# Spreading SSD decays and gate rows by DRAM reads instead of TensorE products, in a one-layer hybrid trunk

## The chip, the cores and the metric

The kernel runs on one core of one Trainium2 chip. A core has five engines that each work through their own list of instructions in order and wait for each other through semaphores: TensorE (PE in the profile, with its weight loads as PEld), VectorE (DVE), ScalarE (ACT), GpSimd (POOL) and SyncE (SP), which here only issues transfers. Transfers between DRAM, where the inputs lie, and the on-chip memory SBUF are done by DMA engines; PE writes its results into PSUM, a small memory of eight banks of 128 x 512 f32 values.

The metric is the device time of the whole kernel in microseconds (us). Before the change it is 1217.26 us, the median of 3 runs (1215.96 to 1217.44). "Time" always means this one number; positions such as "425 us" are microseconds from the start of the profiled execution's span.

## The reference

One layer of a hybrid encoder over 1024 positions of width 1024. What matters here is the state-space group (SSD, 8 heads of width 64) and how its output joins the residual:

```
z, xbc, dt_raw, q, k, v = split(h @ W_in)
dt    = softplus(dt_raw + dt_bias)                 # 1024 x 8
adt   = -exp(a_log) * dt
a_cs  = cumsum(adt) over each chunk
L     = exp(a_cs[l] - a_cs[s])  for s <= l, else 0  # one 'decay' matrix per chunk and head
y     = ((C B^T) * L) @ (xs * dt)                   # inside the chunk
      + exp(a_cs) * (C @ state_before)              # from earlier chunks
state = exp(a_cs[-1]) * state + B^T @ (exp(a_cs[-1] - a_cs) * xs * dt)
y     = (y + d_skip * xs) * silu(z)
y_ssd = y / rms(y) * norm_w
x     = x + g_m * (concat[y_ssd, y_att] @ W_out)    # g_m, g_f: one row of 1024 each, from c
x     = x + g_f * ffn(...)
```

The sequence is handled in 8 tiles of 128 positions, which the kernel calls chunks (c = 0 to 7). All values are f32. Large products are made of three products of a rounded high part and a low rest (names that end in h or H and l or L), so that the result has f32 precision.

## The kernel before, in words

The program runs through the layer once. The stretch that matters lies between about 370 and 525 us:

- **z tiles.** `z_tile(ch, st, wz)` computes columns of `h @ W_in` for tile `st`, first the half `ch = 1` (372 to 398 us, which also holds dt_raw), then the half `ch = 0` (398 to 423 us). PE makes 24 products of 260 columns, ACT and DVE then bring the result out of PSUM into `zs` (lines 656, 657 for half 1, 660, 661 for half 0, the last of which is z times the sigmoid part of silu). Half 0 needs the weights `wzh`, `wzl`, which are loaded and split on ACT and DVE between the halves (lines 82, 83).
- **Gate rows.** g_m and g_f exist as 128 x 8 columns `gcol`. Products by rows need them spread over all 128 partitions. `row_of` does that: DVE multiplies the identity by the columns (line 141), PE multiplies the result by a matrix of ones (line 144), ACT copies it out (line 145). It is called for g_m behind the first z tile and for g_f behind the third. The row of g_m is folded into four parts of W_out by DVE (`wout_fold`, line 612, tiles `wst`, `wos`); its other half stays as `gm1`. The row of g_f goes to DRAM as a full 128 x 1024 tile (`gfd`, line 852) and comes back near the end of the program.
- **dt_prep** (from 398.8 us) computes dt and adt (`sm_dt`, `sm_e`) on DVE and ACT, then three products of adt on PE with a lower triangle `tle`, a strict upper triangle `sgt` and ones, and one exp: `ex3` holds the three decays of 64 columns (`ea`, `de`, `cd`, one column per chunk and head).
- **ssd_pre(c)** makes what chunk c needs: `xdt = xs * dt` (DVE), `xdd = xdt * de` (POOL), the product C B^T (`cb`, masked by `tle`), and the decay matrices of 8 heads. For these, ACT and DVE multiply `tle` by each head's column of adt, high and low part apart (lines 714, 716, 720, tile `rm`), and PE multiplies by the strict triangle `sgtr` (tile `sg`, two products of 512 columns for each of two groups of four heads); ACT takes the exp (line 739) and DVE multiplies by `cb` (line 740, tile `th`).
- **ssd_y(c)** is PE's part: `ydp` (inside the chunk), `yop` (from the state), `stp` (the new state), with POOL making `yy = d_skip * xs` ahead (line 811) and DVE adding up (829 to 832).
- **ssd_norm(c)** multiplies by `zs` (DVE, 837), takes the mean square (ACT 839, POOL 116 and 117) and scales (ACT 841). **ssd_turn(c)** transposes the result on PE into `xps` and copies it into `xs`; `wout_rhs` splits it into `yhl`.
- **wout_half(n)** multiplies `yhl` by the split W_out (tiles `hH`, `hL`) into `wops`: 24 products of 512 columns. Half n of them runs beside chunk n: three steps between the two groups of ssd_pre(c + 1), the rest behind it. So PE's row in the loop is: ydp, yop, stp, turn of the chunk before, products of ssd_pre(c + 1), wops.

PE's order in the loop is the order in which the program writes it (`pe` chains each product to the one before). On the other engines a scheduler places each instruction by its own estimate; `issue_after` and the list `pin` only bound it: the split of W_out (`wout_split`) waits in the order for the instructions in `pin`. Buffers come from pools with a fixed number of copies: `rm` has 2, `xdt` and `xdd` 2 each, the SSD tiles in PSUM 3 banks (`PB`: banks for wops, xps, sg and SSD tiles).

## Time and profile before

| What | us |
| --- | --- |
| time, median of 3 runs | 1217.26 |
| the profiled execution's own time | 1219.3 |
| its span (first to last instruction) | 1217.5 |
| PE busy | 1170.7 |
| VectorE busy | 928.7 |
| ScalarE busy | 598.1 |
| GpSimd busy | 148.6 |
| z tiles, half 1 / half 0 | 372 to 398 / 398 to 423.4 |
| SSD loop, first ydp to the last turn | 425.13 to 521.34 |

All from one profiled execution, on the one core; its mean granted PE clock was 0.991 of full speed. In the rows of a timeline the columns are: start, duration, engine, line, operation, output<-inputs, shape, count of instructions joined in the row, and in brackets the idle time of the engine before it with what ended that. Where several instructions are joined the duration runs from the first start to the last end. PE's products overlap in their pipeline, so a product's own duration is longer than its distance to the next. In the view of waits a row says who waited for whom, in total, how often, and the longest. In the view of stretches each engine's busy time is followed by its count of instructions; the last three numbers are the granted clock, the share of busy DMA and GB/s. In the list of transfers the last number is the median time from issue to landing.

### The profile page before, as it was taken

To read this page: it belongs to the slowest core of one execution; us is meant where nothing else is said; L and a number is where in the kernel's file an instruction comes from. 1 tells how busy PE (TensorE), PEld (TensorE's weight loads), DVE (VectorE), ACT (ScalarE), POOL (GpSimd) and SP (SyncE) were. 2 spreads that over 40 slices of the span, in tenths; PEclk is the share of its full clock that TensorE was granted. 3 is DMA by queue.
4 is the path that set the end of the run, shared out by engine and by line. 5 is a ranking of instruction groups with operands and counts; after the bars stand their busy time and mean duration, and the time that the engine had idled before them with its cause. 6 is when DMAs were issued, how large, how long until landed. Compare 5 with 4: busy or idle time off the path is not lost.

```text
span 1217.5 us, 15642 instructions
## 1 busy us (share of the span) xinstructions
PE 1170.7 (96%) x5802; PEld 977.2 (80%) x5802; DVE 928.7 (76%) x1394; ACT 598.1 (49%) x1001; POOL 148.6 (12%) x174
## 2 busy tenths in 40 slices
PE   5998999989999999999999999999999999999996
PEld 3877887878788978888878888888888888888885
DVE  7846455686696678746999988988889869756986
ACT  4636454674333766676644533344334445433444
POOL 1202242440000134200000000000000000000522
PEclk9999999999999989999999999999999999999999
DMA  9612121311576201141223223322232277734443
GB/s 343 249 57 80 42 70 39 123 48 50 173 261 206 88 14 39 53 150 58 70 96 112 104 95 130 126 76 85 104 130 95 87 277 274 270 120 130 149 137 146
DMA packets 56395, 150.86 MB, mean 124 GB/s; under 512 B 5632, under 2 KB 5760, under 8 KB 54912
## 3 DMA queue, kind: packets, MB, share of 16 engines
q1 hardware_dynamic: 49264, 125.49, 30.5%
q10 hardware_dynamic: 7056, 24.38, 5.0%
q8 instruction: 45, 0.74, 0.2%
q14 instruction: 30, 0.25, 0.1%
HBM read 116.56 MB, written 29.10 MB: 120 GB/s over the span
## 4 chain that ended last, share of the span: by engine, by line
PE 70%; DVE 5%; ACT 1%; issue 1%; DMA 1%; POOL 0%; POOLq 0%; DVEq 0%; ACTq 0%; SPq 0%
PE wops L699 6%; PE dn L78 5%; PE dn L77 5%; PE dn L76 5%; PE uY L76 5%; PE uY L78 5%; PE uY L77 4%; PE uX L78 3%; PE uX L76 3%; PE uZ L77 3%; PE uZ L76 3%; PE uX L77 3%; PE uZ L78 3%; PE s L76 3%; PE s L77 3%; PE s L78 3%
## 5 line engine op out<-in xcount | busy, mean ns | idle before, releaser
L77 PE MATMUL dn<-w 128*128 128x512 f32 x296 | 108.1, 391 | 0.0
L76 PE MATMUL dn<-w 128*128 128x512 f32 x296 | 108.1, 391 | 0.0
L78 PE MATMUL dn<-w 128*128 128x512 f32 x296 | 100.2, 391 | 0.2 <-DVE w L86 0.2
L76 PE MATMUL uY<-tH,w 128*128 128x512 f32 x248 | 97.2, 392 | 0.0
L77 PE MATMUL uY<-tL,w 128*128 128x512 f32 x248 | 97.0, 391 | 0.0
L78 PE MATMUL uY<-tH,w 128*128 128x512 f32 x248 | 96.9, 391 | 0.0
L1427 POOL TENSOR_TENSOR ya<-ya,xs 128x512 f32<-128x512 f32 x4 | 17.2, 4338 | 557.7 <-ACT xs L1423 557.7
L85 ACT ACTIVATE w<-ya 128x1024 fp32r<-128x1024 f32 (+1 forms) x41 | 39.2, 956 | 87.3 <-PE uY L78 84.2
L699 PE MATMUL wops<-hH,yhl 128*128 128x512 f32 x224 | 75.9, 407 | 2.9 <-DVE yhl L86 1.5
L78 PEld LDWEIGHTS dn<-w 128*128 128x128 f32 x296 | 55.4, 188 | 13.2 <-DVE w L86 1.1
L76 PEld LDWEIGHTS dn<-w 128*128 128x128 f32 x296 | 55.5, 188 | 12.4
L77 PEld LDWEIGHTS dn<-w 128*128 128x128 f32 x296 | 55.5, 188 | 12.2
L413 DVE CUSTOM_DVE_ANT_0 p<-s,bias 128x640 f32<-128x640 f32 (+4 forms) x64 | 40.7, 652 | 25.0 <-PE tp L445 9.0
L85 ACT ACTIVATE w<-xs 128x1024 fp32r<-128x1024 f32 (+1 forms) x41 | 39.1, 953 | 37.3 <-PE uY L78 33.3
L419 POOL TENSOR_SCALAR p<-p,st 128x640 f32<-128x640 f32 (+4 forms) x64 | 46.1, 726 | 76.7 <-DVE st L418 66.5
L86 DVE TENSOR_TENSOR pt<-tp,pt 128x512 fp32r<-128x512 f32 (+2 forms) x72 | 42.0, 595 | 16.9 <-ACT pt L85 16.5
L78 PEld LDWEIGHTS uY<-tH,w 128*128 128x128 f32 x248 | 46.6, 188 | 10.4
L76 PEld LDWEIGHTS uY<-tH,w 128*128 128x128 f32 x248 | 46.6, 188 | 10.4
L77 PEld LDWEIGHTS uY<-tL,w 128*128 128x128 f32 x248 | 46.6, 188 | 10.2
L699 PEld LDWEIGHTS wops<-hH,yhl 128*128 128x128 f32 x224 | 42.9, 193 | 12.5 <-DVE yhl L86 1.9
L76 PE MATMUL s<-hH,wh 128*128 128x512 f32 x128 | 50.2, 392 | 1.6 <-DVE ct L520 1.6
L1101 DVE SCALAR_TENSOR_TENSOR a<-cv,pkt,a 128x1023 f32<-128x1023 f32 (+1 forms) x40 | 50.9, 1276 | 0.1
(459 smaller groups left out, 3430.5 us busy)
## 6 DMA issues: line engine op xcount, KB each, us to landing
wos<-in_w_ada_dram SPq DMA_DIRECT2D x25, 512.0 KB, 4.7
gz<-a ACTq DMA_DIRECT2D x10, 1024.0 KB, 4.9
ya<-in_w_up_dram SPq DMA_DIRECT2D x11, 768.0 KB, 4.2
xs<-in_w_up_dram SPq DMA_DIRECT2D x11, 768.0 KB, 4.1
adat<-in_w_ada_dram SPq DMA_DIRECT2D x16, 512.0 KB, 5.7
raws<-in_w_ft_dram SPq DMA_DIRECT2D x14, 512.0 KB, 3.7
gy<-a ACTq DMA_DIRECT2D x10, 512.0 KB, 2.6
qk<-in_x_dram SPq DMA_DIRECT2D x8, 512.0 KB, 6.4
```

The costliest lines, as they stand in the source:

```text
L76: T.matmul(ps, lh, rh, start=start, stop=False, skip_group_check=more)
L77: T.matmul(ps, lh, rl, start=False, stop=False, skip_group_check=more)
L78: T.matmul(ps, ll, rh, start=False, stop=stop, skip_group_check=more)
L85: i = A.activation(hi, src, AF.Copy) if ehi is A else ehi.tensor_copy(hi, src)
L86: return i, elo.tensor_tensor(lo, src, f32(hi), ALU.subtract)
L413: V.tensor_tensor_reduce(out=dst, in0=src, in1=bsl, scale=-1.0, scalar=3e38, op0=ALU.add, op1=ALU.min, accum_out=nm)
L419: G.tensor_scalar(pv_, pv_, rr, 1.0, op0=ALU.mult, op1=ALU.mult)
L699: i = op(*a, **k)
L1101: V.scalar_tensor_tensor(a[:, j:S], c[:, 0:S - j], w[2 - j], a[:, j:S], op0=ALU.mult, op1=ALU.add)
L1427: G.tensor_tensor(src, src, fnr[:, halves[1]], ALU.mult)
```

## The change

Three things change.

1. **Gate rows.** `row_of` goes. `cols_to_dram` instead turns the 8 columns into 8 rows of 128 by one product with the identity, copies them out on ACT and writes the 4 KB to DRAM (`gmd`, `gfd`). Reads whose source is the same 4 KB block for each of the 128 partitions (`rows_from`) then fill the two halves of g_m's spread row, 256 KB each, and, near the end, the 512 KB of g_f. The full-size write of `gfd` goes.
2. **Decays.** The `rm` multiplications and the `sg` products go. `dt_prep` rounds adt to a coarse grid (`ad`, multiples of 2^-6, by adding and subtracting a large number), keeps the rest beside it, makes the cumulative sums of both with one product with `tle`, copies them out and writes the 64 x 128 table of the coarse sums to DRAM (`acd`). A transpose of the same copy gives the sums as columns: the coarse ones in `acc`, and from the fine rest f the factors exp(f) (`sm_t`) and exp(-f) (`sm_t2`). ssd_pre(c) reads its 8 rows of `acd`, spread over all partitions, into `cr` (512 KB, one read per chunk, two buffers), and the decay is the exp of min(cr - acc, 0) of the coarse sums, made by ACT for four heads (Relu with a scale of -1) and by DVE for four. The fine factors are folded elsewhere: exp(-f) into dt and into the skip factor (`sm_p`, which replaces d_skip as POOL's operand), exp(f) into `de` and, by eight new POOL multiplications, into `zs`. `sgtr`, `adh` and `adl` are not needed any more.
3. **Order and banks.** ssd_turn(0) is written ahead of ssd_y(1)'s products instead of behind them. The list `pin` is set back to dt_prep's own copies behind ssd_pre(0). The bank that `sg` had goes to the SSD tiles (4 now), and the z tiles of half 0 use the banks `acc` and `pv` for tiles 0, 1, 6 and 7 instead of 0, 1, 4 and 5.

SP's list changes too: behind the loads of W_out now stand the writes of gmd and gfd and the reads of `rows` and `gm`, before the loads of half 0's z weights; behind the next four loads of W_out stand the write of acd and the reads of cr for chunks 0 and 1; and behind two more loads the other six reads of cr, with the loads of `xr` between them.

```diff
-PB = (2, 2, 1, 3)
+PB = (2, 2, 0, 4)
+GRID = 1.5 * 2.0 ** 17
...
-    def row_of(cols, dst, psp, tag, bufs, ones, tmp):
-        for hh in range(2):
-            t = tmp()
-            ps = psp.tile([P, 512], F32, tag=tag, bufs=bufs, name="rowps")
-            V.tensor_tensor(t.rearrange("p (a b) -> p a b", a=4),
-                            ident.unsqueeze(1).to_broadcast([P, 4, P]),
-                            cols[:, 4 * hh:4 * hh + 4].unsqueeze(2).to_broadcast([P, 4, P]), ALU.mult)
-            T.matmul(ps, ones, t, start=True, stop=True)
-            A.activation(dst[hh], ps, AF.Copy)
+    def cols_to_dram(cols, ps, t, d):
+        T.matmul(ps, cols, ident, start=True, stop=True)
+        A.activation(t, ps, AF.Copy)
+        nc.sync.dma_start(d, t)
...
+    gmd, gfd = (dram.tile([8, P], F32, name=n) for n in ("gmd", "gfd"))
+    acd = dram.tile([64, P], F32, name="acd")
+
+    def rows_from(d, k, n):
+        return d[k:k + n].unsqueeze(0).to_broadcast([P, n, P])
...
-        if st % 4 < 2:
-            ps = psv.tile([P, 512], F32, tag=("acc", "pv")[st % 4], bufs=1, name="zps")[:, 0:260]
+        if st < 2 or st // 2 == (3, 2)[ch]:
+            ps = psv.tile([P, 512], F32, tag=("acc", "pv")[st % 2], bufs=1, name="zps")[:, 0:260]
...
-        pin[:] = [i.ins for i in split(adh, adl, sm["adt"], A, V)]
+        ad, acr = (th512()[:, 0:P] for _ in range(2))
+        V.tensor_scalar(ad[:, 0:64], sm["adt"], GRID, GRID, op0=ALU.add, op1=ALU.subtract)
+        V.tensor_tensor(ad[:, 64:P], sm["adt"], ad[:, 0:64], ALU.subtract)
         dps = tp_tile()
-        for i, m in enumerate((tle, sgt, ones)):
-            T.matmul(dps[:, 64 * i:64 * i + 64], m, sm["adt"], start=True, stop=True)
-        A.activation(ex3, dps[:, 0:192], AF.Exp)
+        T.matmul(dps[:, 192:192 + P], ad, tle, start=True, stop=True)
+        i = A.activation(acr, dps[:, 192:192 + P], AF.Copy)
+        nc.sync.dma_start(acd, acr[0:64])
+        T.transpose(dps[:, 320:320 + P], acr, ident)
+        pin[:] = [i.ins, V.tensor_copy(acc_, dps[:, 320:384]).ins]
+        A.activation(sm["t"], dps[:, 384:448], AF.Exp)
+        A.activation(sm["t2"], dps[:, 384:448], AF.Exp, scale=-1.0)
+        A.activation(sm["ea"], dps[:, 320:384], AF.Exp)
+        for i, m in enumerate((sgt, ones)):
+            T.matmul(dps[:, 64 + 64 * i:128 + 64 * i], m, sm["adt"], start=True, stop=True)
+        A.activation(ex3[:, 64:192], dps[:, 64:192], AF.Exp)
+        V.tensor_tensor(sm["dt"], sm["dt"], sm["t2"], ALU.mult)
+        V.tensor_tensor(sm["de"], sm["de"], sm["t"], ALU.mult)
+        V.tensor_tensor(c8(sm["p"]), c8(sm["t2"]),
+                        pkt[:, DSK:DSK + 8].unsqueeze(1).to_broadcast([P, 8, 8]), ALU.mult)
...
+        G.tensor_tensor(h8(zs[:, c, 0:512]), h8(zs[:, c, 0:512]), hb("t", c), ALU.mult)
+        cr = bcp.tile([P, 8, P], F32, tag="rm", bufs=2, name="cr")
+        nc.sync.dma_start(cr, rows_from(acd, 8 * c, 8))
         for g in range(2):
-            rm = bcp.tile([P, 2, 4, P], F32R, tag="rm", bufs=2, name="rm")
-            hs = slice(c * 8 + 4 * g, c * 8 + 4 * g + 4)
-            for h in range(4):
-                A.activation(rm[:, 0, h, :], tle, AF.Copy, scale=f32(adh)[:, hs.start + h:hs.start + h + 1])
-            if g == 0:
-                V.tensor_tensor(rm[:, 1], tle.unsqueeze(1).to_broadcast([P, 4, P]),
-                                f32(adl)[:, hs].unsqueeze(2).to_broadcast([P, 4, P]), ALU.mult)
-            else:
-                for h in range(4):
-                    A.activation(rm[:, 1, h, :], tle, AF.Copy,
-                                 scale=f32(adl)[:, hs.start + h:hs.start + h + 1])
-            sg = sgp_()
-            for i in range(2):
-                pe(T.matmul, sg, sgtr, rm[:, i].rearrange("p h l -> p (h l)"), start=i == 0, stop=i == 1)
+            for k in range(4 * g, 4 * g + 4):
+                a = acc_[:, 8 * c + k:8 * c + k + 1]
+                if g == 0:
+                    A.activation(cr[:, k], cr[:, k], AF.Relu, scale=-1.0, bias=a)
+                else:
+                    V.tensor_scalar(cr[:, k], cr[:, k], a, 0.0, op0=ALU.subtract, op1=ALU.min)
...
-            pin1 = A.activation(m, sg.rearrange("p (h l) -> p h l", h=4), AF.Exp)
+            pin1 = A.activation(m, cr[:, 4 * g:4 * g + 4], AF.Exp, scale=(-1.0, 1.0)[g])
...
-            row_of(gcol[:, 0:8], (rowb[:, 0:512], gm1), pst, "tp", 2, ones, rm512)
+            cols_to_dram(gcol[:, 0:8], tp_tile()[0:8, 0:P], th512()[0:8, 0:P], gmd)
+            for t, k in ((rowb[:, 0:512], 0), (gm1, 4)):
+                nc.sync.dma_start(t.rearrange("p (a b) -> p a b", a=4), rows_from(gmd, k, 4))
...
-            row_of(gcol[:, 8:16], [rowa[:, h] for h in halves], pst, "tp", 2, ones, rm512)
+            cols_to_dram(gcol[:, 8:16], tp_tile()[0:8, 0:P], th512()[0:8, 0:P], gfd)
...
             dt_prep()
-            pre0 = ssd_pre(0, tp_tile, tp_tile)
             pin0 = list(pin)
+            pre0 = ssd_pre(0, tp_tile)
+            pin[:] = pin0
...
-        G.tensor_tensor(h8(y), h8(xs[:, c, :]),
-                        pkt[:, DSK:DSK + 8].unsqueeze(2).to_broadcast([P, 8, 64]), ALU.mult)
+        G.tensor_tensor(h8(y), h8(xs[:, c, :]), hb("p", c), ALU.mult)
...
-    gfd = dram.tile([P, D], F32, name="gfd")
-    nc.sync.dma_start(gfd, rowa)
...
     for c in range(NT):
+        if c == 1:
+            ssd_turn(*turn)
         y, t = ssd_y(c, *pre)
-        if turn:
+        if c > 1:
             ssd_turn(*turn)
...
-            nc.sync.dma_start(gf, gfd)
+            nc.sync.dma_start(gf.rearrange("p (a b) -> p a b", a=8), rows_from(gfd, 0, 8))
```

How this moves instructions shows at three places. (Line numbers below differ between the two kernels, since the code got longer or shorter above them.) First VectorE, from the split of W_out's first half to chunk 0's sums; `zs` is the last step of a z tile, `hL` the low part of W_out, `yy<-ydp,yy` the first addition of y(0). Before:

```order
549 L86 TENSOR_TENSOR hL_85<-wst,hH_83 128x1024 x2
550 L86 TENSOR_TENSOR hL_85<-wos,hH_83 128x1024
551 L86 TENSOR_TENSOR hL_85<-raws,hH_83 128x1024
552 L661 SCALAR_TENSOR_TENSOR zs<-zt,zps 128x260
553 L86 TENSOR_TENSOR yhl<-ya,yhl 128x512
554 L661 SCALAR_TENSOR_TENSOR zs<-zt,zps 128x260
555 L661 SCALAR_TENSOR_TENSOR zs<-zt,s 128x260 x2
556 L83 SCALAR_TENSOR_TENSOR hL_86<-wos,pkt,hH_84 128x512 x3
557 L829 TENSOR_TENSOR yy<-ydp,yy 128x512
```

After; `cr<-cr,acc` are VectorE's four heads of a chunk's decays, the three rows of it for chunks 0, 1 and 2:

```order
543 L728 TENSOR_SCALAR cr<-cr,acc 128x128 x4
544 L656 SCALAR_TENSOR_TENSOR zs<-zt,s 128x260
...
548 L728 TENSOR_SCALAR cr<-cr,acc 128x128 x4
549 L744 TENSOR_TENSOR th<-th,cb 128x512
...
552 L744 TENSOR_TENSOR th<-th,cb 128x512
553 L656 SCALAR_TENSOR_TENSOR zs<-zt,s 128x260
554 L728 TENSOR_SCALAR cr<-cr,acc 128x128 x4
555 L656 SCALAR_TENSOR_TENSOR zs<-zt,s 128x260
556 L656 SCALAR_TENSOR_TENSOR zs<-zt,zps 128x260 x2
```

The last three z tiles' `zs` now stand behind the decays of chunk 2, and those of chunks 0 and 1 behind the split of W_out. The next place is GpSimd from the first SSD work on. Before:

```order
79 L708 TENSOR_TENSOR xdd<-xdt,ex_2864 128x512 x2
80 L811 TENSOR_TENSOR yy<-xs,pkt 128x512 x2
81 L708 TENSOR_TENSOR xdd<-xdt,ex_2864 128x512
82 L825 TENSOR_TENSOR state_4054<-state_4055,ex_2864 128x512
83 L116 TENSOR_SCALAR st_72<-st_72 128x1
```

After:

```order
79 L719 TENSOR_TENSOR zs<-zs,sm_t 128x512 x4
80 L717 TENSOR_TENSOR xdd<-xdt,ex_2863 128x512 x2
81 L719 TENSOR_TENSOR zs<-zs,sm_t 128x512 x3
82 L815 TENSOR_TENSOR yy<-xs,sm_p 128x512 x2
83 L719 TENSOR_TENSOR zs<-zs,sm_t 128x512
84 L717 TENSOR_TENSOR xdd<-xdt,ex_2863 128x512
85 L828 TENSOR_TENSOR state_4048<-state_4049,ex_2863 128x512
86 L117 TENSOR_SCALAR st_72<-st_72 128x1
```

All eight `zs` multiplications stand before or at chunk 1, seven of them ahead of chunk 0's `yy`. The third place is PE where chunk 0 goes over into chunk 1; `xps<-ident,yy` is the turn of y(0). Before:

```order
2054 L699 MATMUL wops<-hL_85,yhl 128x512
2055 L699 MATMUL wops<-hH_83,yhl 128x512
2056 L699 MATMUL ydp<-xdt,th 128x64 x8
2057 L699 MATMUL yop<-state_4055,ct_2848 128x256
2058 L699 MATMUL yop<-state_4055,ct_2849 128x256
2059 L699 MATMUL stp<-xdd,cb 128x256 x2
2060 L699 MATMUL xps<-ident,yy 128x128 x4
2061 L699 MATMUL sg<-rm,sgtr 128x512 x2
```

After:

```order
2050 L708 MATMUL wops<-hL_85,yhl 128x512
2051 L708 MATMUL wops<-hH_83,yhl 128x512
2052 L708 MATMUL xps<-ident,yy 128x128 x4
2053 L708 MATMUL ydp<-xdt,th 128x64 x8
2054 L708 MATMUL yop<-state_4049,ct_2848 128x256
2055 L708 MATMUL yop<-state_4049,ct_2849 128x256
2056 L708 MATMUL stp<-xdd,cb 128x256 x2
2057 L708 MATMUL xps<-ct_2848,bt_2846 128x128
```

The turn of y(0) now stands ahead of chunk 1's ydp, and the `sg` products are gone.

More of the change, by code (lines that the diff above doesn't have):

```diff
@@ L554, in tile_block @@
     sm["nx"], sm["adt"] = sm["p"], sm["e"]
-    adh = bcp.tile([P, 64], F32R, name="adh")
-    adl = bcp.tile([P, 64], F32R, name="adl")
+    acc_ = bcp.tile([P, 64], F32, name="acc")
     ex3 = bcp.tile([P, 192], F32, name="ex3")
@@ L561, in tile_block @@
     tle, ones = tle1[:, 0, :], tle1[:, 1, :]
-    sgtr = bcp.tile([P, P], F32R, name="sgtr")
+    sgt = bcp.tile([P, P], F32, name="sgt")
     wos = bcp.tile([P, 3, D], F32, name="wos")
@@ L585, in tile_block @@
                     pattern=[[1, P]], channel_multiplier=-1)
-    G.affine_select(out=sgt_, in_=ones, compare_op=ALU.is_gt, fill=0.0, base=0,
+    G.affine_select(out=sgt, in_=ones, compare_op=ALU.is_gt, fill=0.0, base=0,
                     pattern=[[-1, P]], channel_multiplier=1)
-    V.tensor_copy(sgtr, sgt_)
-    sgt = f32(sgtr)
     for ft in range(4):
@@ L701, in pe, with ssd_pre @@
             chain[0] = i.ins
-    def ssd_pre(c, xp_, sgp_, between=None):
+    def ssd_pre(c, xp_, between=None):
         cs = slice(c * P, (c + 1) * P)
```

7 lines of the change are left out of this document (1 added, 6 removed).

## The prediction

> **What bounds the kernel now.** I read the page first, then the waits of TensorE (PE) over the stretch that the change touches, then the stretches of 10 or 20 us with their clock, then the timelines.
>
> ```profile
> span 1217.5 us, 15642 instructions
> PE 1170.7 (96%) x5802; PEld 977.2 (80%) x5802; DVE 928.7 (76%) x1394; ACT 598.1 (49%) x1001; POOL 148.6 (12%) x174
> PE 70%; DVE 5%; ACT 1%; issue 1%; DMA 1%; POOL 0%; POOLq 0%; DVEq 0%; ACTq 0%; SPq 0%
> ```
>
> PE is busy for 96% of the span and holds most of the chain that ended last. So a change is worth the PE work it removes, plus the PE waits it removes, less those it makes. The waits between 360 and 530 us, and the clock:
>
> ```profile
> PE ydp L699 <- DVE zs L661: 1.7, 1, 1.7
> PE wops L699 <- DVE yhl L86: 1.5, 1, 1.5
> PE wops L699 <- ACT yhl L85: 1.4, 1, 1.4
> PE xps L699 <- ACT yy L841: 0.6, 1, 0.6
> ...
> 420.00:430.00 10.00, 8.26 (x54) 7.57 (x53) 7.78 (x14) 8.56 (x20) 2.67 (x3) 0.86 0.17 53
> 430.00:440.00 10.00, 10.00 (x55) 8.75 (x54) 7.91 (x11) 5.81 (x17) 4.30 (x4) 0.97 0.01 2
> 440.00:460.00 20.00, 17.07 (x82) 14.00 (x81) 13.57 (x20) 11.12 (x30) 7.12 (x8) 0.83 0.07 27
> 460.00:480.00 20.00, 20.00 (x113) 17.40 (x112) 16.81 (x23) 14.18 (x39) 8.45 (x10) 1.00 0.15 53
> ```
>
> Four waits, 5.2 us in all. The third number from the right is the granted clock: it falls behind the waits. In 420 to 440 it loses 10 x 0.14 + 10 x 0.03 = 1.7 us behind the one wait of ydp; in 440 to 460 it loses 20 x 0.17 = 3.4 us behind two waits of wops. So a PE wait of 1.4 to 1.7 us costs about 1.7 us more after it. From 460 on PE never waits, so there each us taken from PE is a us of the span. The chunks, by the first matmul of each ydp:
>
> ```profile
> 425.13 2.00 PE L699 MATMUL ydp<-xdt,th 128*128 128x64 f32 x16 [1.74 <-DVE zs L661]
> ...
> 436.61 1.89 PE L699 MATMUL ydp<-xdt,th 128*128 128x64 f32 x16
> ...
> 453.72 1.89 PE L699 MATMUL ydp<-xdt,th 128*128 128x64 f32 x16
> 464.77 1.89 PE L699 MATMUL ydp<-xdt,th 128*128 128x64 f32 x16
> ...
> 486.88 2.19 PE L699 MATMUL ydp<-xdt,th 128*128 128x64 f32 x16
> ...
> 499.01 1.22 PE L699 MATMUL ydp<-xdt,th 128*128 128x64 f32 x10
> ```
>
> A chunk is worth 464.77 - 453.72 = 11.05 us. Chunk 0 took 11.48, chunk 1 took 17.11 (6.06 over: 2.93 of waits, the rest the clock), chunk 5 took 12.13 (1.08 over, with the 0.6 wait in it).
>
> **The change, part by part. Row spreading for the gates.** The f32 matmuls of row_of leave PE:
>
> ```profile
> 384.56 0.28 PE L77 MATMUL zps<-wzl,hH 128*128 128x260 f32 x1
> 384.68 1.02 PE L144 MATMUL rowps<-gt,tle 128*128 128x512 f32 x2
> 385.14 0.68 PE L78 MATMUL zps<-wzh,hL 128*128 128x260 f32 x1
> 385.66 0.28 PE L76 MATMUL zps<-wzh,hH 128*128 128x260 f32 x1
> ```
>
> The z matmuls follow each other by 0.12, so a call of L144 costs 385.66 - 384.56 - 2 x 0.12 = 0.86 us, four calls 3.4. The two 8x128 products that come instead are one f32 matmul of 128 columns each, at most 0.4 together by the same rows. Net -3.0 us of PE before 395. What the rows feed now waits for a write and a read in series:
>
> ```profile
> 386.37 2.36 DVE L612 TENSOR_TENSOR wst<-wst,rows 128x1024 f32<-128x1024 f32 x2
> 388.65 2.35 DVE L612 TENSOR_TENSOR wos<-wos,rows 128x1024 f32<-128x1024 f32 x2
> ...
> 396.66 1.43 DVE L83 SCALAR_TENSOR_TENSOR wzl<-raws,wzh 128x520 fp32r<-128x520 f32 x2 [1.67 <-ACT wzh L82]
> ...
> qk<-qk SPq DMA_DIRECT2D x32, 128.0 KB, 2.2
> xr<-in_x_dram SPq DMA_DIRECT2D x8, 512.0 KB, 4.3
> dna<-gy SPq DMA_DIRECT2D x1, 512.0 KB, 10.8
> ```
>
> With the first product at about 384.7 and its copy out at 385.4, a write of 2.2 and a read of 4.3 bring the rows at 391.9; the two pairs of multiplies (4.7) end at 396.6, and wzl, which stands behind them in VectorE's (DVE's) order, is at its old time. PE comes to the second half of the z tiles 3.0 us earlier and waits there for wzl and for the PSUM tile that DVE frees behind the same multiplies. So I take nothing from this part at its place. It would be 3.0 if the cover were there, and below zero by some 2 us if the transfers queue as the 10.8 row did.
>
> **The start of chunk 0.** ydp(0) waits for the last z tile's product on DVE. That product stands, in DVE's and ScalarE's (ACT's) order, behind the relus on the third broadcast table cr(2), whose read waits until cr(0) is used up. The chain starts where sm_e ends:
>
> ```profile
> 405.30 0.22 DVE L680 SCALAR_TENSOR_TENSOR sm_e<-sm_dt,na 128x64 f32<-128x64 f32 x1
> ...
> 415.12 2.00 ACT L85 ACTIVATE hH<-wst 128x1024 fp32r<-128x1024 f32 x2
> ...
> 418.91 0.37 ACT L660 ACTIVATE zt<-zps 128x260 f32<-128x260 f32 x1
> 419.18 1.27 ACT L714 ACTIVATE rm<-tle,adh 128x128 fp32r<-128x128 f32 x4
> ...
> 424.66 0.42 DVE L661 SCALAR_TENSOR_TENSOR zs<-zt,s 128x260 f32<-128x260 f32 x1 [0.51 <-ACT zt L660]
> ```
>
> 405.5; two DVE operations of 0.22 make it 406.0; the product with tle comes at the next place in PE's order, about 2 us on; its copy on ACT ends at 408.6; the write (2.2) 410.8; the read of cr(0) (4.3) 415.1. There ACT has the four hH splits (4.0 from their row) and the relus, so the exps of cr(0) end at about 418.5. cr(2) is then issued and lands at 422.8; four relus of the L714 kind 1.27, zt 0.37, zs 0.42: 424.9. That is within 0.2 us of where ydp(0) starts now. I take 0; the whole of the 3.0 us and of the four sg-type products that leave this stage (4 x 0.46, rows below) is swallowed, and PE idles 1.74 + 1.8 = 3.5 us just before ydp(0), the 3.0 lying at the gates. No row shows a broadcast read of one 4 KB block: 4.3 is the nearest by shape (128 rows of 4 KB), 10.8 the far end. If neither wait stood, the z work itself would end 3.0 + 1.8 = 4.8 us earlier.
>
> **Chunk 0 and the turn.** The sg products leave PE:
>
> ```profile
> 428.73 0.85 PE sg L699 x2
> ...
> 432.87 0.46 PE sg L699 x2
> ```
>
> 0.85 + 0.46 = 1.31 off chunk 0, the second at full clock. The four transposes of y(0) now stand before ydp(1), and wait for y(0), which begins with POOL's yy(0):
>
> ```profile
> 423.36 2.04 POOL L811 TENSOR_TENSOR yy<-xs,pkt 128x512 f32<-128x512 f32 x2 [10.71 <-PE s L77]
> ...
> 431.33 1.49 POOL L825 TENSOR_TENSOR state<-state,ex 128x512 f32<-128x512 f32 x1
> ...
> 427.26 0.68 DVE L829 TENSOR_TENSOR yy<-ydp,yy 128x512 f32<-128x512 f32 x1
> ...
> 434.42 0.72 ACT L841 ACTIVATE yy<-yy,st 128x512 f32<-128x512 f32 x1 [2.15 <-POOL st L117]
> ```
>
> From DVE's first addition to the scaled y it took 435.14 - 427.26 = 7.9 us. POOL now has seven of the eight new zs multiplies ahead of yy(0); I give each the 1.49 of the state multiply, which has the same shape and head broadcast. The last two of the seven wait for z tiles that come after cr(2), at 424.5, so they end at 427.9 at the latest end of that, yy(0) at 429.4, y(0) at 437.3, and ydp(1) starts at 437.8 after four transposes, taken at the 0.12 of the z matmuls. PE would be there at 425.1 + 11.48 - 1.31 = 435.3: a wait of 2.0. Chunk 0's term is 437.8 - 436.61 = +1.2. If POOL started on time, it would be -1.3 + 0.5 = -0.8.
>
> **Chunk 1.** Its two waits go, since the turn is a chunk ahead of its wops; what is late next is only the clock behind the new wait. A standard chunk 11.05, less 0.92 of sg (2 x 0.46), less 0.5 of moved transposes, plus 1.7 of clock: 11.3 against 17.11, -5.8.
>
> The Trainium skill, page "TensorE: Matmul & The Clock Gate", section "Part 1: The HAM clock gate", puts the fall to half clock after an idle window of about 3.4 us. By that a wait of 2.0 would lose no clock, and the sum would be 1.7 us better; here the clock fell after 1.74, so the row decides.
>
> **Chunks 2 to 6** lose 0.92 each: -4.6. Chunk 7 has no sg. ACT loses per chunk eight L714 and four L720 copies for four relus of the same size, DVE one rm product for four 128x128 operations, so neither is later than now; I take half of chunk 5's 1.08, -0.5. The reads of cr have a whole chunk of time. POOL's zs multiplies are all done in the first chunks. The 512 KB write of gfd goes and its read at the end becomes a broadcast: 0, since PE does not wait on it now.
>
> **The sum:** 0 + 1.2 - 5.8 - 4.6 - 0.5 = -9.7. The profiled execution took 1219.3 (span 1217.5 and 1.8 around it), 2.0 above the median of the runs; I put the difference on the median: 1217.3 - 9.7 = 1207.6, said as 1208. Its own range is 1204 to 1212.
>
> **Rivals.**
> - *The covers hold* (0.13): PE does not wait at ydp(0) (3.0 + 1.74 come back), or not at the turn (2.0 and 1.7 of clock): each is worth 4 to 5 us, so one of them makes the gain 14, near 1203. Against it: a write of 2.2 and two reads of 4.3 in series fill just the time there is.
> - *Waits form again* (0.15): the gates hold DVE and PE at 396 and cost clock (1.7), and y(0) comes 2 us later, since POOL's operations take 2.0 rather than 1.5 (row 429.38 below is such a one). Then 9.7 - 3.7 leaves 6.0, and 3 if the clock falls there too: 1211 to 1214, say 1213.
>
> ```profile
> 429.38 2.00 POOL L708 TENSOR_TENSOR xdd<-xdt,ex 128x512 f32<-128x512 f32 x1 [3.98 <-DVE xdt L707]
> ```
>
> - *Reading one block 128 times halves the rate* (0.07): the window
>
> ```profile
> 380.00:390.00 10.00, 10.00 (x74) 8.79 (x72) 7.51 (x14) 3.12 (x6) 0.00 (x0) 1.00 0.65 213
> ```
>
>   moved 213 GB/s; at half of that 512 KB lasts 4.9 us instead of 2.5, so each read lands 2.4 later, ydp(0) waits for two in series, +4.9, leaving 4.8: 1213. The Trainium skill, page "DMA: Bandwidth & Descriptors", section "Latency and other measured facts", tells of such a halved rate where the rows of the partitions lie at large powers of two, and calls the cause an inference; no run here shows it.
> - *The other side: the broadcast read is slow* (0.20). At the 10.8 of the crowded row, two reads in series put ydp(0) 13 us later: -9.7 + 13 = +3.3, 1221. It decides from a landing of 4.3 + 9.7 / 2 = 9.2 us up. Steady chunks stay unharmed until a read and its use, over two buffers, exceed two chunks, about 17 us; beyond that every chunk is late. For it: no such read in the trace; against it: the 4.3 of xr, whose 128 rows have the same length, and a share of busy DMA of only 0.07 to 0.17 in 420 to 460.
>
> **Numbers.** The forecast has 0.45. 0.2% (2.4 us) is what a measurement of this kernel can tell from no change. Faster: 0.45 + 0.13 + most of the two 1213 cases (0.18) = 0.76; same: their edges and the slow read's, 0.07; slower: the rest of the slow read, 0.17. The range goes from 1201, past the covers' 1203, to 1221, the slow read's own time.
>
> **What would show it.** sg, rm and rowps are gone from PE; cr lands in 4 to 5 us; ydp(0) starts at 424 to 426 with a wait of some 3.5 us on zs; PE waits about 2 us at the xps of y(0) for ACT's yy; no wait at chunk 1's wops; chunks 2 to 6 take 10.13 us. A cr landing above 9.2 us, or a wait inside the steady chunks, makes the prediction wrong; ydp(0) before 422 makes it too small.

## The result, and the profile after

The changed kernel takes 1212.51 us (median of 20 runs, 1210.5 to 1217.32) against 1217.14 (20 runs of the kernel before beside them): a ratio of 0.9964, 95% interval 0.9954 to 0.9975. It is faster by 4.4 us by that ratio (4.6 by the medians), which is less than half of the 9.7 us that were forecast. The profiled execution's span fell by 5.3 us, from 1217.5 to 1212.2. Of all executions reported below, two of the last kernel (e18), at 1302 and 2972 us, ran far slower than the others of the same kernel and are left out of its time.

The head of the changed kernel's page:

```profile
span 1212.2 us, 15576 instructions
PE 1161.0 (96%) x5767; PEld 970.0 (80%) x5767; DVE 930.4 (77%) x1418; ACT 579.5 (48%) x938; POOL 159.0 (13%) x182
```

Its waits from 360 to 530 us, those of PE (us in total, times, longest):

```profile
PE ydp L708 <- DVE zs L656: 5.4, 1, 5.4
PE xps L708 <- ACT yy L844: 1.6, 2, 1.3
PE ydp L708 <- DVE th L744: 1.0, 1, 1.0
```

And three stretches (their length, the busy time and instructions of PE, PEld, DVE, ACT and POOL, the granted clock, the DMA share and GB/s):

```profile
420.00:430.00 10.00, 4.64 (x32) 4.43 (x31) 8.85 (x18) 3.25 (x10) 7.16 (x6) 0.75 0.15 54
430.00:440.00 10.00, 10.00 (x42) 8.70 (x42) 8.16 (x11) 6.44 (x12) 6.40 (x7) 0.74 0.14 52
440.00:460.00 20.00, 18.43 (x108) 15.58 (x107) 19.74 (x34) 10.61 (x25) 8.55 (x11) 1.00 0.22 79
```

PE is busy 9.7 us less (1161.0 for 1170.7). That this is also the forecast's figure is chance: the PE work that the prediction took away adds up to 11.7 us (3.0 + 4 x 0.46 + 1.31 + 0.92 + 4.6), and its 9.7 is a sum with waits and clock in it. PE waits 5.4 us at ydp(0), where it waited 1.7, and the clock is low up to 435 us. The two waits of wops in chunk 1 are gone. The chunks, in PE's timeline:

```profile
428.06 3.68 PE L708 MATMUL ydp<-xdt,th 128*128 128x64 f32 x16 [5.36 <-DVE zs L656]
...
441.84 0.66 PE L708 MATMUL xps<-ident,yy 128*128 128x128 f32 x4 [1.27 <-ACT yy L844]
442.34 1.90 PE L708 MATMUL ydp<-xdt,th 128*128 128x64 f32 x16
...
452.00 2.00 PE L708 MATMUL ydp<-xdt,th 128*128 128x64 f32 x16
...
504.38 1.89 PE L708 MATMUL ydp<-xdt,th 128*128 128x64 f32 x16
```

| stretch | before | forecast change | after | measured change |
| --- | --- | --- | --- | --- |
| up to ydp(0) | 425.13 | 0 | 428.06 | +2.9 |
| chunk 0 | 11.48 | +1.2 | 14.28 | +2.8 |
| chunk 1 | 17.11 | -5.8 | 9.66 | -7.4 |
| chunks 2 to 6 | 56.34 | -5.1 | 52.38 | -4.0 |
| ydp(7) to the end | 707.4 | 0 | 707.8 | +0.4 |
| sum | | -9.7 | | -5.3 |

(Chunks 2 to 6 end at ydp(7), 510.06 before. The first z product, ahead of all edits, came 1.15 us later in the profile after, 373.45 for 372.30, so only 1.8 of the 2.9 lie behind it. In e5 and e13 below, which have the same lists up to ydp(0), the stretch from there to ydp(0) took 55.4 and 55.7 us, for 52.8 before: 2.6 and 2.9 more.)

What sets ydp(0) shows in VectorE's timeline of the changed kernel:

```profile
411.13 0.23 DVE L686 COPY acc<-tp 128x64 f32<-128x64 f32 x1 [1.38 <-PE tp L685]
411.27 2.35 DVE L87 TENSOR_TENSOR hL<-wst,hH 128x1024 fp32r<-128x1024 f32 x2
413.54 2.07 DVE L87 TENSOR_TENSOR hL<-wos,hH 128x1024 fp32r<-128x1024 f32 x1
415.53 2.06 DVE L87 TENSOR_TENSOR hL<-raws,hH 128x1024 fp32r<-128x1024 f32 x1
417.51 1.65 DVE L728 TENSOR_SCALAR cr<-cr,acc 128x128 f32<-128x128 f32 x4
...
420.29 1.65 DVE L728 TENSOR_SCALAR cr<-cr,acc 128x128 f32<-128x128 f32 x4
...
422.61 1.28 DVE L716 TENSOR_TENSOR xdt<-xs,sm_dt 128x512 f32<-128x512 f32 x2
...
424.74 2.92 DVE L728 TENSOR_SCALAR cr<-cr,acc 128x128 f32<-128x128 f32 x4
427.59 0.41 DVE L656 SCALAR_TENSOR_TENSOR zs<-zt,s 128x260 f32<-128x260 f32 x1
```

GpSimd's timeline of the same kernel, its multiplications of `zs` in the same microseconds:

```profile
412.86 5.63 POOL L719 TENSOR_TENSOR zs<-zs,sm_t 128x512 f32<-128x512 f32 x3 [119.46 <-ACT sm_t L687]
```

The same split in VectorE's timeline before, with no GpSimd work beside it:

```profile
418.48 1.22 DVE L86 TENSOR_TENSOR hL<-wos,hH 128x1024 fp32r<-128x1024 f32 x1
```

From 411 us to the last zs ahead of ydp(0) VectorE has no gap of note. The split `hL` that took 1.22 before takes 2.06 while GpSimd multiplies `zs`, and the decays stand ahead of the last zs. From the copy into `acc` to ydp(0) it is 16.93 us here, and 16.93 again in the three runs below that leave this list as it is (e5, e6 and e13), wherever the list starts. The reads, the suspect of the forecast, are innocent: cr(0) is there at 414.3 (415.1 in the forecast), and they land in 3.9 us:

```profile
cr<-acd SPq DMA_DIRECT2D x8, 512.0 KB, 3.9
```

### The profile page after: what moved, and what is told of

Same layout as the page of the kernel before. It is cut to its first block, busy times and chain, and to the rows that moved or that the text cites. A ratio compares the mean times of both kernels' runs of the same rounds, so it can differ in the third digit from the quotient of the medians.

```text
span 1212.2 us, 15576 instructions
## 1 busy us (share of the span) xinstructions
PE 1161.0 (96%) x5767; PEld 970.0 (80%) x5767; DVE 930.4 (77%) x1418; ACT 579.5 (48%) x938; POOL 159.0 (13%) x182
## 4 chain that ended last, share of the span: by engine, by line
PE 65%; DVE 7%; DMA 2%; ACT 2%; issue 1%; POOL 1%; POOLq 0%; SPq 0%; ACTq 0%; DVEq 0%
PE dn L79 5%; PE dn L78 5%; PE dn L77 5%; PE uY L77 5%; PE uY L79 5%; PE uY L78 5%; PE wops L708 4%; PE uX L79 3%; PE uZ L78 3%; PE uX L77 3%; PE uX L78 3%; PE uZ L77 3%; PE uZ L79 3%; PE s L77 2%; PE s L78 2%; PE s L79 2%
## 5 line engine op out<-in xcount | busy, mean ns | idle before, releaser
L708 PE MATMUL wops<-hH,yhl 128*128 128x512 f32 x224 | 72.9, 398 | 0.0
L79 PEld LDWEIGHTS dn<-w 128*128 128x128 f32 x296 | 55.4, 188 | 13.2 <-DVE w L87 1.1
L412 ACT ACTIVATE p<-p,st 128x640 f32<-128x640 f32 (+4 forms) x64 | 44.1, 690 | 14.0 <-DVE st L409 13.8
```

What stands on the lines that cost most here:

```text
L79: T.matmul(ps, ll, rh, start=False, stop=stop, skip_group_check=more)
L412: A.activation(pv_, pv_, AF.Exp, scale=-1.0, bias=nm, accum_out=rs)
L708: i = op(*a, **k)
```

## The experiments

Theory A: VectorE's list, slowed by GpSimd, sets ydp(0); the turn alone brought the gain. Times are medians; the ratio is against the kernel before, run beside them (1216 to 1217 us), with its 95% interval. The changed kernel's is 0.9964 (0.9954 to 0.9975). "The turn" is the turn of y(0), "the list" an engine's instructions in their order.

**The parts apart.** The turn alone (e4):

```diff
     for c in range(NT):
+        if c == 1:
+            ssd_turn(*turn)
         y, t = ssd_y(c, *pre)
-        if turn:
+        if c > 1:
             ssd_turn(*turn)
```

> The kernel before with one edit: the turn of y(0) ahead of chunk 1's products. In the kernel before y(0) is ready at 435.1, ahead of PE's 436.6, so no wait forms there; the two waits of wops (1.43 and 1.50) and the slow clock behind them (about 3) should go: chunk 1 falls from 17.1 to 11 to 12 us and the time by 5 to 6 us, as much as the whole change brought. The rival: y(0) comes later or the split behind it still is late, then half of it, 2 to 3 us.

1212.39 us, 0.9957 (0.9942 to 0.9973). One moved line of four transposes brings all that the whole change brings. Its chunk 1:

```profile
436.93 1.90 PE L699 MATMUL ydp<-xdt,th 128*128 128x64 f32 x16
447.56 1.89 PE L699 MATMUL ydp<-xdt,th 128*128 128x64 f32 x16
```

10.63 us against 17.11; chunk 0 gave back 2.1 of it (13.58 against 11.48). The wait at ydp(0) is the same 1.74 us as before, but the clock lost 3.4 us behind it and not 1.7 (rows in the last section). The counterpart, the changed kernel with the turn back in its old place (e5, the same diff reversed):

> The changed kernel with the turn of y(0) put back behind chunk 1's ydp, yop and stp, so that only the DRAM spreading of gates and decays is left of the change. Theory A (the spreading's PE savings are eaten at ydp(0), the turn is what gained): PE's 1.27 us wait at the turn goes, but wops of chunk 1 waits for the split of y(0) again, by 2 to 4 us, and the clock falls again: the time is 3 to 6 us above the changed kernel's 1212.5, about that of the kernel before (1216 to 1218). The rival (each part brings its share): 1 to 2 us above the changed kernel, still 2 us or more below the kernel before.

1215.88 us, 0.9995 (0.9986 to 1.0004): spreading gates and decays through DRAM is worth nothing by itself, though it takes about 10 us off PE. The waits of wops are back, in its list of waits:

```profile
PE wops L708 <- DVE yhl L87: 2.4, 1, 2.4
PE wops L708 <- ACT yhl L86: 0.7, 1, 0.7
```

**The gate rows.** In e6 `row_of` is back in the changed kernel; in e9 the kernel before has the turn and the gate rows, without the decays.

```diff
-            cols_to_dram(gcol[:, 0:8], tp_tile()[0:8, 0:P], th512()[0:8, 0:P], gmd)
...
+            row_of(gcol[:, 0:8], (rowb[:, 0:512], gm1), pst, "tp", 2, ones, rm512)
```

> The changed kernel with the gate rows spread by the four f32 products again, as before; decays and turn as changed. Theory A: the 3 us of PE that the gate rows save lie ahead of a wait of 5.4 us at ydp(0) that VectorE's list sets, so PE comes to it 3 us later and waits 3 us less, and the time stays within 1.5 us of the changed kernel. It may even fall, since VectorE has its gate multiplications done 5 us earlier and a shorter idle time costs less clock. The rival (the 3 us of PE are gained): 2 to 3.5 us slower than the changed kernel.

> The kernel before with the turn of y(0) moved and the gate rows spread through DRAM; the decays are made on PE as before. In this kernel the wait at ydp(0) is 1.74 us behind PE's own last z tile, so what PE saves ahead of it should reach the end, unless the gate multiplications come late: theory A (the gate part was worth nothing in the changed kernel only because ydp(0) waited for VectorE) expects 1 to 3 us below the run with the turn alone, 1209.5 to 1211.5. The rival (the gate rows come too late by themselves: PE waits for the PSUM tile or for wzl, 1 to 3 us, and loses clock): no better than the turn alone, 1212 or more.

e6: 1213.23, 0.9965 (0.9952 to 0.9979); e9: 1211.32, 0.9957 (0.9944 to 0.9971), no different from the turn alone. (The 1211.32 of e9 lies in the range that its theory A gave, but the kernel before was 0.8 us faster beside it than beside the turn alone; by the ratios nothing was gained.) So the gate rows' 3 us show in neither time. Where the changed kernel loses them is not shown: e6's expectation put them into the wait at ydp(0), but that wait is 5.4 us with `row_of` too. In e9 PE waits where the prediction had put it, for a PSUM tile and wzl behind the late multiplications, 1.4 us of the 3.0. Its waits:

```profile
PE ydp L696 <- DVE zs L658: 1.5, 1, 1.5
PE zps L76 <- DVE zs L654: 1.2, 1, 1.2
...
PE zps L77 <- DVE wzl L83: 0.2, 1, 0.2
```

And VectorE's row of the multiplication that waits for the gate rows' read:

```profile
392.25 2.36 DVE L607 TENSOR_TENSOR wst<-wst,rows 128x1024 f32<-128x1024 f32 x2 [4.55 <-DMA rows<-gmd]
```

The read brings the rows within 0.4 us of the forecast's 391.9.

**GpSimd's multiplications.** Left out (e1), and put alone, by ones, into the kernel with the turn (e10):

```diff
-        G.tensor_tensor(h8(zs[:, c, 0:512]), h8(zs[:, c, 0:512]), hb("t", c), ALU.mult)
```

> The changed kernel without the eight GpSimd multiplications of zs by exp(f); that factor is left out of the result. Theory A (VectorE's list sets the start of chunk 0, and GpSimd's multiplications slow VectorE while they run): the three slow low-part splits of W_out (2.0 to 2.1 us each) fall to about 1.2, the VectorE decays of chunk 2 from 2.9 to 1.6 for four, ydp(0) starts 2.5 to 4 us earlier than 428.06, and the time falls by 3 to 6 us against the changed kernel. Theory B (the reads of the table set the start): VectorE's operations get shorter, but ydp(0) starts at most 1.3 us earlier and the time falls by less than 2 us. Theory C (only the place of chunk 2's decays in the list counts): ydp(0) 1.3 us earlier, from those decays alone.

> The kernel before with the turn of y(0) moved and eight GpSimd multiplications of zs by ones, of the same size and shape as the changed kernel's and at the same place in GpSimd's list; nothing else of the change. It prices the suspected cost by itself. Theory A: the 1.22 us splits of W_out become 2 us or more beside them, yy(0) starts 3 us or more later, PE waits at ydp(0) or at the turn, and the time is 3 to 6 us above the run with the turn alone (1212.4), so 1215 to 1218. The rival (GpSimd's multiplications cost only beside the changed VectorE list): within 1.5 us of 1212.4.

e1: 1208.44, 0.9926 (0.9911 to 0.9942), 0.4% below the changed kernel. e10: 1215.68, 0.9998 (0.9988 to 1.0008), 0.4% above the turn alone. The cost of the eight multiplications is shown from both sides, some 4 to 5 us. VectorE's rows in e1, with no GpSimd work until the last row:

```profile
411.94 1.22 DVE L87 TENSOR_TENSOR hL<-wos,hH 128x1024 fp32r<-128x1024 f32 x1
...
414.21 0.87 DVE L727 TENSOR_SCALAR cr<-cr,acc 128x128 f32<-128x128 f32 x4
...
420.10 3.50 DVE L727 TENSOR_SCALAR cr<-cr,acc 128x128 f32<-128x128 f32 x4 [0.16 <-DMA cr<-acd]
```

2.06 is 1.22 again, and four decays 0.87 instead of 1.65. The four of chunk 2 at 420.10 take 3.50, beside GpSimd's xdd and yy, where 1.6 had been expected. From `acc` to ydp(0) it is 14.46 us instead of 16.93; most of the gain lies in chunk 0, 11.66 us instead of 14.28, where the clock is back at 1.00 in 430 to 440 (0.74 in the changed kernel). In e10 ydp(0) did not start later: there GpSimd's first multiplications end before the splits begin. Its loss lies behind it, in VectorE's second splits (three in 4.51 instead of 2.08) and two waits for th. So the cost is real, but the place that the expectation gave for e10 was half wrong. VectorE's row of it in e10's timeline:

```profile
423.18 4.51 DVE L83 SCALAR_TENSOR_TENSOR hL<-wos,pkt,hH 128x512 fp32r<-128x512 f32 x3 [0.19 <-ACT hH L82]
```

And the wait of PE:

```profile
PE ydp L699 <- DVE th L742: 1.2, 2, 0.8
```

**The order at ydp(0).** The decays of chunks 1 and 2 behind the last z step (e2), and the splits behind chunk 0's decays (e3, the line `pin[:] = pin0` left out):

```diff
+                with tc.issue_after(zlast[g]) if c in (1, 2) else ExitStack():
                     if g == 0:
                         A.activation(cr[:, k], cr[:, k], AF.Relu, scale=-1.0, bias=a)
...
```

> The changed kernel with the decays of chunks 1 and 2 kept, in the order of ScalarE and VectorE, behind the last z tile's last steps; nothing else is edited. Theory A (VectorE's list is the chain): 1.6 us of chunk 1's decays and 2.9 us of chunk 2's leave the list ahead of the last zs, so ydp(0) starts 3.5 to 4.5 us earlier than 428.06, the wait of 5.4 us falls to 1 to 2 us, the clock falls less, and the time is 4 to 7 us below that of the changed kernel. Theory B (the table's reads): the wait for cr(2) no longer stands ahead of ydp(0), so it too expects an earlier start, by 3 us, and the same sign. A rival D expects nothing in the end: the decays of chunks 1 and 2 then run beside chunk 0 and hold up y(0) and th(1), so that ydp(1) waits as long as ydp(0) did, and the time falls by less than 1.5 us.

> The changed kernel without the line that sets the pin list back: the split of W_out's first half stands behind chunk 0's decays again, as in the kernel before. Theory A: the same VectorE work still stands ahead of the last zs, only in another order (th(0) 4 to 6 us earlier, the last zs where it was), so ydp(0) starts within 1.5 us of 428.06 and the time is within 2 us of the changed kernel. Theory E (the reset of the pin list is what made the start late, since 6.5 us of splits now stand ahead of the decays): ydp(0) starts 3 us earlier or more and the time falls by 4 us or more.

e2: 1214.22, 0.9974 (0.9963 to 0.9986); e3: 1216.89, 0.9997 (0.9984 to 1.001). In e2 the wait at ydp(0) fell to 1.5, as A said, but the time did not fall, and rival D was right in the main: PE waits 3.8 at the turn, since the decays now stand ahead of y(0). e3 was worse than A allowed (4.4 at ydp(0) and 4.9 at the turn), and E was wrong on the time.

**Multiplications in their chunks** (e7), with late decays (e8), with all decays on ScalarE (e11), and both (e12):

```diff
-        G.tensor_tensor(h8(y), h8(xs[:, c, :]), hb("p", c), ALU.mult)
+        i = G.tensor_tensor(h8(y), h8(xs[:, c, :]), hb("p", c), ALU.mult)
+        with tc.issue_after(i.ins):
+            G.tensor_tensor(h8(zs[:, c, 0:512]), h8(zs[:, c, 0:512]), hb("t", c), ALU.mult)
```

> The changed kernel with each of GpSimd's eight multiplications of zs moved behind the yy of its chunk, in the loop; the same work. Theory A: as without them at all up to ydp(0): the splits at 1.2 us, a start of chunk 0 some 4 us earlier than in the changed kernel against the end of the z tiles, and 1207 to 1210 us in all; in the chunks GpSimd has 1.0 to 1.5 us more, which it has time for. The rival: the multiplications then slow VectorE in every chunk, new waits of 0.5 us or more appear in chunks 2 to 6, and the time is 1211 or more.

> Both moves: the multiplications of zs in their chunks, and the decays of chunks 1 and 2 behind the last z tile's last steps. Theory A with the lesson of the run with late decays alone: ydp(0) no longer waits at all or under 1 us; the 16 decay operations then run with GpSimd less busy, at 0.2 to 0.4 us each on VectorE, so y(0) comes in time and PE waits at the turn under 1.5 us: 1203 to 1207 us. The rival D: the decays stand ahead of y(0)'s steps on VectorE, PE waits 3 us or more at the turn and the clock falls: no better than with the zs multiplications moved alone.

> The changed kernel with the multiplications of zs in their chunks and all eight decays of a chunk made by ScalarE; VectorE makes none. Theory A (VectorE's list is the chain up to and through chunk 0): the decays of 0.2 to 0.9 us each leave it, ydp(0) starts 2 us earlier than with the zs multiplications moved alone, the wait of th in the later chunks goes, and the time is 1206 to 1209. The rival: ScalarE's list takes its place, since the decays of chunk 2 stand ahead of its last z steps: no better than 1211.

> The same, with ScalarE's decays of chunks 1 and 2 behind its last z step. Theory A: neither engine has the decays of later chunks ahead of ydp(0); it starts as PE is through with the z tiles, PE waits under 1 us at the turn, and the time is 1203 to 1207, the lowest of all runs. The rival: chunk 0's own list on VectorE (the second half of the W_out split, 8 operations of 0.7 us, ahead of y(0) and th) is the bound by now, PE waits 2 us or more at the turn, and the time is within 1.5 us of the run before.

| run | us | ratio (interval) | wait at ydp(0) | at the turn |
| --- | --- | --- | --- | --- |
| e7 | 1211.28 | 0.9954 (0.9941 to 0.9966) | 3.5 | 1.2 |
| e8 | 1211.18 | 0.9956 (0.9943 to 0.9969) | 0.9 | 2.5 |
| e11 | 1214.92 | 0.9990 (0.9980 to 1.0001) | 0.8 | 8.0 |
| e12 | 1212.55 | 0.9971 (0.9962 to 0.9980) | 0.8 | 5.4 |

e7 takes 1.9 us off the wait at ydp(0) and leaves the turn's as it was; its time is the changed kernel's within the intervals, and a wait of 1.4 for th is left in a later chunk. In the other three ydp(0) is nearly free, and the turn takes over with 2.5 to 8.0 us. All four missed the times that theory A gave. In e12 VectorE is done with y(0) at 427.3, but its square stands on ScalarE behind eight splits and the decays. ScalarE's row of the square:

```profile
432.98 0.63 ACT L841 ACTIVATE yt<-yy 128x512 f32<-128x512 f32 x1
```

And the wait of the turn:

```profile
PE xps L708 <- ACT yy L843: 5.4, 1, 5.4
```

**Place or amount?** In e13 to e15 the splits of W_out's second half stand behind the scaling of y(0): in the changed kernel, in e8 and in e12, the decays of chunk 2 behind it too in the last two.

```diff
-        A.activation(y, y, AF.Copy, scale=r)
+        i = A.activation(y, y, AF.Copy, scale=r)
+        return i.ins
...
-                ssd_norm(c, y, t, at)
+                nrm[:] = [ssd_norm(c, y, t, at)]
...
-                    pin[:] = zlast
+                    pin[:] = [nrm[0], zlast[1]]
                     wout_split(j, wt[j])
```

> The changed kernel with one edit: the splits of W_out's second half stand behind the scaling of y(0) in the lists of ScalarE and VectorE. ydp(0) still starts late (wait of about 5 us), since nothing ahead of it is touched. If place is the limit: y(0) is scaled 2 to 3 us earlier, PE's wait at the turn (1.3 us) goes, and the time falls by 1 to 2 us to 1210.5 to 1211.5. If the amount of work is the limit: the splits are late for wops of chunk 1, a new wait of 1 us or more appears there, and the time is 1212 or more.

> With the zs multiplications in their chunks, the decays of chunk 1 behind the last z step and those of chunk 2 behind y(0)'s scaling, and the splits behind it too. If place is the limit: the wait at ydp(0) is about 1 us, the one at the turn under 0.5 us (2.5 us with its slow clock in the run without this order), and the time is 1205 to 1208, below every run so far. If the amount of work is the limit: PE waits 2 us or more for the splits at wops of chunk 1 or for th, and the time stays at 1210 or more.

> The same with all decays on ScalarE. If place is the limit: the 5.4 us wait at the turn goes and the time is 1204 to 1208. If ScalarE's amount of work is the limit: its 8 splits (5.2 us), 16 decays (5 us) and the copies of chunk 0 fill more than the chunk's 10 to 11 us, PE waits 2 us or more for yhl at wops of chunk 1, and the time is above that of the run with the decays shared.

e13: 1218.6, 1.0015 (1.0001 to 1.0028); e14: 1217.84, 1.0012 (1.0003 to 1.0022); e15: 1214.21, 0.998 (0.9968 to 0.9992). e13 and e14 are slower than the kernels they were made from; e15 can't be told from e12 by its interval. In e13 the wait at the turn is gone, and new ones stand at wops of chunk 1, where the second case had put one:

```profile
PE wops L708 <- DVE yhl L87: 4.3, 1, 4.3
PE wops L708 <- ACT yhl L86: 1.6, 1, 1.6
```

e14 waits as long at wops (4.3 and 1.3) and still 3.7 at ydp(0); e15 waits 3.2 at the turn and 2.6 and 0.9 at wops.

**The table for later chunks only**, on top of e9: from chunk 2 (C0 = 2, e16), that with the last four splits behind y(0) (e17), and from chunk 3 with the same late splits (C0 = 3, e18). Chunks before C0 keep rm and sg.

```diff
+        if c >= C0:
+            cr = bcp.tile([P, 8, P], F32, tag="rm", bufs=2, name="cr")
+            nc.sync.dma_start(cr, rows_from(acd, 8 * c, 8))
...
```

> The run with the turn and the gate rows, and the DRAM table for the decays of chunks 2 to 7 alone; chunks 0 and 1 have the sg products on PE and no factor exp(f); zs is multiplied in its chunk. If the saving is real and was lost only at the start: the six chunks' sg products leave PE (6 x 0.92 = 5.5 us) and no wait is added at ydp(0), so 1206 to 1208.5 against 1211.3. If it is always paid back: new waits of VectorE or ScalarE in chunks 1 to 6 take as much, and the time is 1210.5 or more. Here the splits of W_out's second half stand ahead of y(0) on VectorE (seven of eight), which may cost up to 2 us at the turn.

> The same, with the last four of those eight splits behind the scaling of y(0). If the saving is real: the wait at the turn is under 0.7 us and the time is 1205 to 1208. If always paid back: 1210.5 or more.

> The same with the table from chunk 3 on: one chunk less of saving (0.92 us), but no decays of the table beside chunk 1. If chunk 1 has room, 0.5 to 1.5 us slower than the run with the table from chunk 2; if chunk 1 is full too, faster than it by 1 us or more.

e16: 1212.63, 0.996 (0.9945 to 0.9975); e17: 1217.26, 1.0002 (0.9986 to 1.0018); e18: 1214.8, 0.9981 (0.9964 to 0.9998). All three wait 5.4 us at ydp(0) again. By the order of the rows that is a side effect of this edit: dt_prep's new products stay in one of two shared PSUM tiles until their column sums are copied out at 415.3, so chunk 0's own products come late (PE's `tp<-ct,bt` at 415.4) and th with them. VectorE's row of th in e16:

```profile
419.53 0.69 DVE L771 TENSOR_TENSOR th<-th,cb 128x512 f32<-128x512 f32 x1 [1.50 <-ACT th L770]
```

And the wait of PE:

```profile
PE ydp L716 <- DVE zs L662: 5.4, 1, 5.4
```

So these runs don't tell whether a table for the later chunks would pay. From ydp(1) to ydp(7) e16 took 64.0 us (441.47 to 505.50) against e9's 67.4 (435.50 to 502.88): 3.4 of the 5.5 us of sg work reached the time there; a wait of 1.4 for th and slower chunks took the rest. The same kernel with a PSUM tile of its own for the table was not tried. None of the versions that compute the whole result beats the changed kernel by more than the intervals; e6 to e9, e12, e16 and the turn alone equal it.

## Why the prediction was right or wrong

**Right:** the sign; that the gate rows bring nothing, in part for the reason given (waits of 1.4 us in e9, but only 0.2 for wzl in the changed kernel); that the start of chunk 0 hangs on VectorE's last zs and swallows what PE saves ahead of it; that PE waits for y(0) at the turn; that chunk 1's two waits go. The broadcast read lands in 3.9 us (4.3 taken), so the two rivals on the read fall. That two rivals stood at 1213, where the time came out, is luck: neither came about in its own terms. The read is not halved, the clock is 1.00 from 380 to 400, where the gates were to cost some, and the turn's wait got shorter than forecast, not longer.

**The step that failed** is "The start of chunk 0": its term 0 was +2.9 in the profile, 1.8 of it behind the first z product. The working followed the reads and ScalarE, and these came nearly as forecast (cr(2) at 423.4, for 422.8); the same step let VectorE work at its durations of before and with nothing in its way. There the four splits end at 417.6, where cr(0) is ready at 414.3, and the decays of chunks 0, 1 and 2, xdt (moved behind the table's factor) and th all stand in a row behind them, 16.9 us from `acc` to ydp(0). The four decays of chunk 2, 2.92 us between the last two zs ahead of ydp(0), were given no time at all. The runs show both parts of the cost: without GpSimd's multiplications (e1) the list is 14.5 us and the time falls by 4 us, and with them moved into the chunks and the decays off VectorE (e11) it is 11.8. The row to see it in was in the trace before: a VectorE operation on 128x512 that takes 0.68 alone takes 1.53 beside GpSimd.

```profile
L716 DVE TENSOR_TENSOR rm<-tle,adl x8: 678/1525/1528, 407.2 to 494.0; 128x512 fp32r<-128x512 f32 x8
```

The Trainium skill, page "SBUF — State Buffer", section "SBUF: two separate sides", says that a VectorE operation with two inputs from SBUF and a GpSimd operation that reads SBUF take turns at a shared pair of ports, an exclusive lock for a whole instruction; that fits the 1.22 and 2.06 of e1 and the changed kernel, where the splits `hL` have two inputs.

**Sized wrong beside it:** chunk 0's term, +1.2, was +2.8. It assumed the same clock as before at its start (1.7 us); with PE idle for 5.4 us ydp took 3.68 instead of 2.00, and from its start to the first wops went 6.42 us (428.06 to 434.48) instead of 5.38 (425.13 to 430.51), though the 0.85 of sg were no longer in it. The wait at the turn (2.0 forecast, 1.3 measured) came by another path than the one forecast, so that it came out near is partly luck. GpSimd's yy(0) ended at 432.1 instead of 429.4, but y(0) waited for VectorE, whose first addition stood behind two splits of W_out:

```profile
432.59 2.97 DVE L84 SCALAR_TENSOR_TENSOR hL<-wos,pkt,hH 128x512 fp32r<-128x512 f32 x2
435.49 0.68 DVE L832 TENSOR_TENSOR yy<-ydp,yy 128x512 f32<-128x512 f32 x1
```

Chunk 1's term was 1.6 too small a gain: the turn's wait of 1.27 cost no clock. The gain of chunks 2 to 6 was 1.1 too large: the sg products gave their 0.92 per chunk (10.11 from 462.71 to 472.82 instead of 11.05), but two waits came back, 1.0 for th in chunk 4 and 0.3 for y. "Neither is later than now" was wrong for VectorE there, and a wait inside the steady chunks was one of the prediction's own signs of being wrong. Two slips did not move the sum: "From 460 on PE never waits" overlooks the 0.6 that the same view lists, and four `sg`-type products at the 0.46 of two are 0.92 us, not 4 x 0.46.

**Still open:** why chunk 0's second wait can't be cleared by order. The runs show that what is taken from ydp(0) comes back at the turn, and from there at wops. That VectorE is simply full in chunk 0 fits that (it is busy 8.2 to 8.9 us of each 10 between 410 and 440; ScalarE is not, with 3.3 of 10 in 420 to 430), but this is argued and not shown: only one order out of many was tried each time. The changed PSUM banks, a third part of the change, were not tested apart.

## What to carry to other kernels

Price moved work on the engine that receives it, in its place in that engine's list and beside its neighbours: 10 us taken off the busiest engine were worth nothing by themselves, since much of the work that replaced them stood on the engine that PE already waited for at the start of the loop. Test the parts of a change apart: here one moved line held the whole gain. And when a wait vanishes, look for the next one in the same chunk before counting the gain.

## What the runs showed of the hardware that was not expected

- **VectorE beside GpSimd.** One small operation (TENSOR_SCALAR, 128x128 f32) took from 0.27 to 1.08 us in one kernel, by what GpSimd did meanwhile:

```profile
L728 DVE TENSOR_SCALAR cr<-cr,acc x32: 273/276/1079, 417.5 to 483.2; 128x128 f32<-128x128 f32 x32
```

- **A wait's price in clock is no constant.** The same wait of 1.74 us at ydp(0) cost 10 x 0.14 + 10 x 0.03 = 1.7 us of clock in 420 to 440 before and 10 x 0.30 + 10 x 0.04 = 3.4 us in the turn alone (e4); 1.54 at the same place in e9 and 1.27 at the changed kernel's turn cost none. The rows of e4, then e9's first:

```profile
420.00:430.00 10.00, 8.26 (x41) 7.50 (x40) 7.31 (x12) 7.66 (x15) 3.27 (x3) 0.70 0.06 22
430.00:440.00 10.00, 10.00 (x55) 8.65 (x54) 7.57 (x11) 6.91 (x19) 4.11 (x5) 0.96 0.01 2
...
420.00:430.00 10.00, 8.46 (x60) 7.74 (x60) 7.79 (x15) 8.57 (x20) 3.25 (x3) 1.00 0.17 53
```

  The changed kernel's 5.36 left PE at half speed for some 7 us more. A fixed price per wait, as the prediction took, is too simple.
- **A read of one 4 KB block by all 128 partitions** costs about what an ordinary 512 KB read does: 3.9 us, beside 3.5 (`xr`) and 3.7 (`raws` from `in_w_ft`) on the same page.
